# Conv columns of a streaming-encoder block moved from direct projections into seven-product units, with the recurrence two chunks at a time

## The chip, the cores and the metric

The kernel runs on one core of a Trainium2 chip. A core has TensorE (matmul, PE in the profile), VectorE (DVE), ScalarE (ACT), GpSimd (POOL) and SyncE (SP), which here issues nearly all DMAs; each engine takes its own instructions in order. The metric is the device time of one launch in microseconds: the median of three runs of the kernel before is 801.97 us (801.75 to 802.11).

## The reference

One block of a hybrid encoder on 512 frames of width 2048. The input is normalised, projected by one matrix, and split into nine parts. Four of them, 1024 columns each, make a gated short convolution; the others make a gated linear attention in chunks of 64 frames. Both results go through one output matrix, are added to the input and normalised again.

```python
h = rms_norm(x, norm_g)
ch, cb, cc, cz, gq, gk, gv, gr, gd = split(h @ w_in)   # 4 x 1024, 512, 512, 1024, 1024, 16
# short convolution: u = cc * ch, causal, 3 taps
y_conv = cb * (conv_b + sum(conv_w[j] * u[t - 2 + j])) * silu(cz)
# linear attention, 4 heads, chunks of 64 frames
glog = log_sigmoid(gd @ w_up + b_gate) / 16
b = cumsum(glog, within a chunk)
k_dec = gk * exp(b_end - b)
state = exp(b_end) * state + k_dec.T @ gv               # chunk after chunk
o = (gq / sqrt(128)) @ state                            # every frame reads its own chunk's state
y_gla = rms_norm(o, per head) * gla_norm_g * silu(gr)
out = rms_norm(x + concat(y_conv, y_gla) @ w_out) * final_g
```

## The kernel before, in words

All arithmetic is float32. Each matmul operand is split into a high part (a cast to the type TensorE multiplies) and a low part (the difference), and a product is three matmuls: high by high, low by high, high by low. ScalarE makes the high parts, VectorE the low ones (`split`, L117 to L119). A weight tile is 128 x 1024 elements (512 KB): it is loaded into one of eight raw buffers (`load_raw`, RAWBUFS = 8) and split into one of four pairs of high and low buffers (SPLITBUFS = 4). Small tiles of 128 x 512 come from one pool of 44 buffers (`t2`, `t2r`). PSUM has eight banks in two pools of four, `acc` and `aux`.

The stages, in order:

- *Token-major projection* (`tm`, L264): the decay gate's input, k and v, with frames on the partitions.
- *Projection units* (`ft_unit`): each makes 128 columns for 512 frames, with columns on the partitions: 16 blocks of the contraction x 3 matmuls = 48 matmuls of 512 columns, from two weight tiles. There are 28: four for q, sixteen for the first half of the conv columns (four blocks of z, b, c, h, `conv_block`), eight for r (`r_block`). After each half unit `step()` advances the generator `gla_steps`, which lays the recurrence in small pieces beside them, one chunk at a time: `chunk_state` (k and v put so that the high part of a chunk lies on 64 partitions and its low part on the other 64, so that one matmul adds both; then the state update and its split), two half units later `chunk_out` (q by the state). After each second chunk `out_norm` normalises a token tile and `out_transpose` turns it into the eight tiles `oT`. `r_block` multiplies silu(r) by `oT` and stores the product to `y_raw` in DRAM.
- *Quarter sums* (`quarter_sums`): for the seven-product units, sums and differences of quarters of the scaled input, four lots of two 512 KB loads, sixteen VectorE sums in all, split again; one lot each after r blocks 0, 2, 4 and 6. `place_third` puts one of the differences over a part of the input that is no longer read.
- *Seven-product units* (`st_unit`): a 512 x 1024 output block from seven products of half-size blocks in place of eight (products pa, pb, pc, then pd, pe, pa, pf in four rounds; 48 matmuls each, 336 in all). Three products take weights as they are, four take sums of weight tiles that VectorE makes (`mix`). Two such units make the second half of the conv columns, a third one, later, half of the output projection.
- *Output projection* (`po`, `part`), with the conv blocks of the second half transposed in between (`conv_tail`: eight transposes, then taps on ScalarE and VectorE), the third unit, and the final norm.

The program is written in one order; a scheduler then puts each engine's instructions into an order by its own estimates, so that a transpose or a split can stand among the matmuls of another stage. Buffers of the pools are handed out at that point too: a load waits until the buffer's last reader is done. Some names in the rows that follow: `hhi` and `hlo` are the high and low parts of the input, `raw_qx` the loads of the quarter sums, `qs` the sums, `qp` their splits, `c` the output tiles of a unit.

Of the kernel before, what the change touches and what calls it, by code (L numbers as in the profile page):

```python
# [13 lines left out]
P = 128  # L14
# [27 lines left out]
PRE = 4  # L42
# [8 lines left out]
def hybrid_block(ctx: ExitStack, tc: tile.TileContext, xT, x, params, w_tm, w_ft, w_st, w_up, b_gate, w_out, final_g, out):  # L51
# [57 lines left out]
    r2B = t2("r2B")  # L109
# [179 lines left out]
    nc.vector.tensor_mul(out=r2B, in0=rB, in1=rB)  # L289
# [58 lines left out]
    state = [None, None]  # L348

    def stack(src, rows, swap, name, both):  # L350

        a = t2r(f"{name}_a")
        nc.scalar.copy(out=a[rows, :], in_=src[rows, :])
        hi = a[rows, :].bitcast(F32)
        if not both:
            nc.vector.tensor_sub(out=a[swap, :], in0=src[rows, :], in1=hi)
            return a
        b = t2r(f"{name}_b")
        nc.scalar.copy(out=a[swap, :], in_=src[rows, :])
        nc.vector.tensor_sub(out=b[rows, :], in0=src[rows, :], in1=hi)  # L360
        nc.vector.tensor_sub(out=b[swap, :], in0=src[rows, :], in1=hi)
        return a, b

    split_state = [None, None]

    def chunk_state(n):
        tt, j = divmod(n, 2)
        rows = slice(j * CHUNK, (j + 1) * CHUNK)
        swap = slice((1 - j) * CHUNK, (2 - j) * CHUNK)
        kh, kl = stack(kv[tt][0], rows, swap, f"k{n}", True)  # L370
        for pr in range(2):
            vs = stack(kv[tt][1 + pr], rows, swap, f"v{n}_{pr}", False)
            u = aux(f"u{n}_{pr}")
# [5 lines left out]
            st = t2(f"s{n}_{pr}")  # L379
            if state[pr] is None:  # L380
                nc.vector.tensor_copy(out=st, in_=u)
            else:
                for i in range(2):
                    hh = 2 * pr + i
                    vsl = slice(i * HV, (i + 1) * HV)
                    nc.vector.scalar_tensor_tensor(
                        out=st[:, vsl], in0=state[pr][:, vsl], scalar=decay[:, hh, n : n + 1],
# [147 lines left out]
    for _ in steps:  # L535
        pass
# [503 lines left out]
```

## Time and profile before

| | us |
|---|---|
| median of 3 runs | 801.97 |
| the profiled execution | 801.89 |
| its span, first to last instruction | 799.7 |
| TensorE busy | 789.5 |
| VectorE busy | 514.6 |
| ScalarE busy | 352.4 |
| GpSimd busy | 38.1 |
| projection units with the recurrence, from 142 to 472 us of the span | 330 |
| first two seven-product units, 472 to 624 us | 152 |

Times in the profile are counted from the first instruction of the span. A matmul's listed duration (0.39 us for 512 columns) is longer than its step to the next one, since matmuls are pipelined; what one costs is read from the distance of starts. The same holds on VectorE and ScalarE by a little. A count after an x stands for instructions merged into one row.

### The profile page before, as it was taken

Reading aid. Unit: us, or ns where it says so; the run is one execution under the profiler, and the core shown is the slowest. Engines: PE = TensorE matmul, PEld = TensorE weight load, DVE = VectorE, ACT = ScalarE, POOL = GpSimd, SP = SyncE. Lnnn points to the kernel's source line nnn. Section 1 sums busy time; section 2 is a strip of 40 time slices with the busy share of each in tenths; the row PEclk is TensorE's granted clock in tenths of the full one; section 3 lists DMA queues with packets and bytes.
Section 4 is the critical chain, followed back from the end, with each engine's and each line's share of the span. In section 5 each row is a group of like instructions: output and inputs, shape, how many; then the busy total and the mean of one; then the engine's idle time right before and its main releaser. Section 6 shows DMA issues by size and latency. Waiting matters only on the chain.

```text
span 799.7 us, 9962 instructions
## 1 busy us (share of the span) xinstructions
PE 789.5 (99%) x3784; PEld 681.4 (85%) x3784; DVE 514.6 (64%) x672; ACT 352.4 (44%) x538; POOL 38.1 (5%) x42
## 2 busy tenths in 40 slices
PE   9999999999999999999999999999999999999996
PEld 9999999888888888788888888888888888888885
DVE  7543242465566566565555577969887998997923
ACT  6542212454445444455344355435445444644504
POOL 1000000000000000000000000000000000003601
PEclk9999999999999999999999999999999999999998
DMA  9963333322222222322355555564665359658105
GB/s 317 313 258 99 107 127 110 106 80 86 100 80 94 104 72 101 105 93 80 100 177 184 173 193 180 192 209 137 235 209 185 106 179 360 200 208 285 32 1 210
DMA packets 43171, 123.60 MB, mean 155 GB/s; under 512 B 5186, under 2 KB 7234, under 8 KB 43124
## 3 DMA queue, kind: packets, MB, share of 16 engines
q1 hardware_dynamic: 42868, 122.96, 45.4%
q8 instruction: 29, 0.48, 0.2%
q14 instruction: 18, 0.15, 0.1%
q10 hardware_dynamic: 256, 0.02, 0.0%
HBM read 115.61 MB, written 7.34 MB: 154 GB/s over the span
## 4 chain that ended last, share of the span: by engine, by line
PE 93%; issue 3%; DVE 1%; ACT 1%; POOL 0%; DMA 0%; ACTq 0%; POOLq 0%; DVEq 0%
PE tm L264 17%; PE ft L159 11%; PE ft L160 11%; PE ft L161 11%; PE pa L616 8%; PE pf L616 4%; PE pe L616 4%; PE pd L616 4%; PE pc L616 4%; PE pb L616 4%; PE po L159 3%; PE po L161 3%; PE po L160 3%; PE warm L87 1%; PE tp L433 0%
## 5 line engine op out<-in xcount | busy, mean ns | idle before, releaser
L159 PE MATMUL ft<-hhi,hi_ft 128*128 128x512 f32 x448 | 174.9, 390 | 0.0
L161 PE MATMUL ft<-hhi,lo_ft 128*128 128x512 f32 x448 | 174.7, 390 | 0.0
L160 PE MATMUL ft<-hlo,hi_ft 128*128 128x512 f32 x448 | 174.6, 390 | 0.0
L118 ACT CAST hi_ft<-raw_ft 128x1024 fp32r<-128x1024 f32 x56 | 58.9, 1052 | 120.0 <-PE ft L160 65.4
L119 DVE TENSOR_TENSOR lo_ft<-raw_ft,hi_ft 128x1024 fp32r<-128x1024 f32 x56 | 68.4, 1224 | 51.9 <-ACT hi_ft L118 51.5
L161 PEld LDWEIGHTS ft<-hhi,lo_ft 128*128 128x128 f32 x448 | 84.1, 188 | 17.5
L159 PEld LDWEIGHTS ft<-hhi,hi_ft 128*128 128x128 f32 x448 | 84.2, 188 | 17.0 <-issue 0.2
L160 PEld LDWEIGHTS ft<-hlo,hi_ft 128*128 128x128 f32 x448 | 84.2, 188 | 16.9
L118 ACT CAST hi_sq_t<-raw_sq 128x1024 fp32r<-128x1024 f32 x48 | 50.5, 1054 | 69.8 <-PE pa L616 14.9
L119 DVE TENSOR_TENSOR lo_sq_t<-raw_sq,hi_sq_t 128x1024 fp32r<-128x1024 f32 x48 | 59.5, 1244 | 15.2 <-ACT hi_sq_t L118 15.0
L665 DVE TENSOR_TENSOR raw_sq<-raw_sq,raw_sq 128x1024 f32<-128x1024 f32 x48 | 58.4, 1221 | 10.0 <-DMA raw_sq<-in_w_st 9.8
L119 DVE TENSOR_TENSOR lo_tm<-raw_tm,hi_tm 128x776 fp32r<-128x776 f32 x24 | 23.2, 966 | 58.4 <-ACT hi_tm L118 55.1
L118 ACT CAST hi_st<-raw_st 128x1024 fp32r<-128x1024 f32 x36 | 38.0, 1054 | 50.4 <-PE pb L616 14.7
L264 PE MATMUL tm<-hi_tm,hhi 128*128 128x388 f32 x256 | 56.5, 343 | 0.0
L264 PE MATMUL tm<-hi_tm,hlo 128*128 128x388 f32 x256 | 55.8, 340 | 0.0
L264 PE MATMUL tm<-lo_tm,hhi 128*128 128x388 f32 x256 | 55.4, 338 | 0.0
L119 DVE TENSOR_TENSOR lo_st<-raw_st,hi_st 128x1024 fp32r<-128x1024 f32 x36 | 43.6, 1222 | 15.5 <-ACT hi_st L118 15.3
L118 ACT CAST hi_tm<-raw_tm 128x776 fp32r<-128x776 f32 x24 | 20.2, 842 | 67.8 <-PE tm L264 64.5
L264 PEld LDWEIGHTS tm<-hi_tm,hhi 128*128 128x128 f32 x256 | 46.5, 190 | 0.0
L264 PEld LDWEIGHTS tm<-hi_tm,hlo 128*128 128x128 f32 x256 | 46.3, 189 | 0.0
L264 PEld LDWEIGHTS tm<-lo_tm,hhi 128*128 128x128 f32 x256 | 46.0, 188 | 0.0
L159 PE MATMUL po<-hi_wo,yh 128*128 128x512 f32 (+1 forms) x104 | 39.6, 381 | 0.0
(284 smaller groups left out, 1319.2 us busy)
## 6 DMA issues: line engine op xcount, KB each, us to landing
raw_ft<-in_w_ft SPq DMA_DIRECT2D x56, 512.0 KB, 3.3
raw_sq<-in_w_st SPq DMA_DIRECT2D x32, 512.0 KB, 3.7
raw_st<-in_w_st SPq DMA_DIRECT2D x24, 512.0 KB, 3.9
raw_tm<-in_w_tm SPq DMA_DIRECT2D x24, 388.0 KB, 5.0
raw_sq<-in_w_out SPq DMA_DIRECT2D x16, 512.0 KB, 4.2
raw_wo<-in_w_out SPq DMA_DIRECT2D x13, 512.0 KB, 3.8
raw_st<-in_w_out SPq DMA_DIRECT2D x12, 512.0 KB, 8.2
rawx<-in_xT SPq DMA_DIRECT2D x16, 256.0 KB, 4.8
```

The costliest lines, as they stand in the source:

```text
L87: nc.tensor.matmul(wps[:, 0:P], lhsT=ones, rhs=ones, start=True, stop=True)
L118: nc.scalar.copy(out=hi, in_=full)
L119: nc.vector.tensor_sub(out=lo, in0=full, in1=hi.bitcast(F32))
L159: nc.tensor.matmul(ps, lhsT=ah, rhs=bh, start=first, stop=False)
L160: nc.tensor.matmul(ps, lhsT=ah, rhs=bl, start=False, stop=False)
L161: nc.tensor.matmul(ps, lhsT=al, rhs=bh, start=False, stop=last)
L264: nc.tensor.matmul(pst[tt][:, 0:TMC], lhsT=a[:, tt * P : (tt + 1) * P], rhs=w, start=kt == 0 and k == 0, stop=kt == KT - 1 and k == 2,)
L616: nc.tensor.matmul(ps[t], lhsT=fs[t][part_], rhs=ww[:, sl], start=first and c == 0 and r == 0 and k == 0, stop=last and c == STC - 1 and r ...
L665: nc.vector.tensor_tensor(out=dst, in0=x0, in1=x1, op=op)
```

## The change

All 4096 conv columns now go through seven-product units: four of them, two for each half (w_st is laid out for four; `st_source` takes w_st for u < 4). `conv_block` and its sixteen projection units are gone, so that twelve projection units are left, q and r. The first half's conv blocks are finished by `early_tail`, inside the third unit, in the two banks that this unit uses later for pd; the transposes and taps of both halves share `conv_transposed`.

The recurrence handles two chunks in one step: `chunk_splits` splits a whole 128-frame tile of k and v; `pair_state` multiplies each chunk on its own 64 partitions with three matmuls per head; `pair_out` makes both chunks' output and the norm, whose scaling has moved from VectorE to ScalarE. It runs beside q and r alone. Since `oT` isn't ready when r is, `r_block` stores silu(r) to `r_raw` in DRAM; `gated_rows`, after the first unit, loads it, multiplies by `oT` and stores to `y_raw`. All four quarter sums stand behind r blocks 6 and 7.

```diff
-    def stack(src, rows, swap, name, both):
...
-    def chunk_state(n):
...
+    def chunk_splits(tt):
+        kv_split[tt] = [split_small(kv[tt][j], f"kv{tt}_{j}") for j in range(3)]
+
+    def pair_state(tt):
+        kp = kv_split[tt][0]
         for pr in range(2):
+            vp = kv_split[tt][1 + pr]
+            us = [aux(f"u{2 * tt + j}_{pr}") for j in range(2)]
             for i in range(2):
                 hh = 2 * pr + i
                 ksl, vsl = slice(hh * HK, (hh + 1) * HK), slice(i * HV, (i + 1) * HV)
-                nc.tensor.matmul(u[:, vsl], lhsT=kh[:, ksl], rhs=vs[:, vsl], start=True, stop=False)
-                nc.tensor.matmul(u[:, vsl], lhsT=kl[:, ksl], rhs=vs[:, vsl], start=False, stop=True)
...
+                for k, (a, b) in enumerate(((0, 0), (0, 1), (1, 0))):
+                    for j in range(2):
+                        rows = slice(j * CHUNK, (j + 1) * CHUNK)
+                        nc.tensor.matmul(
+                            us[j][:, vsl], lhsT=kp[a][rows, ksl], rhs=vp[b][rows, vsl], start=k == 0, stop=k == 2
+                        )
+            for j in range(2):
...
+                state[pr] = st
+                split_state[n, pr] = split_small(st, f"sp{n}_{pr}")
...
+    def pair_out(tt):
+        o = [t2(f"o{tt}_{pr}") for pr in range(2)]
+        for j in range(2):
+            chunk_out(2 * tt + j, o)
+        out_norm(tt, o)
+        return o
...
-                nc.vector.tensor_scalar(
-                    out=o[pr][:, vsl], in0=o[pr][:, vsl], scalar1=ro[:, hh : hh + 1], scalar2=None, op0=ALU.mult
-                )
+                nc.scalar.activation(o[pr][:, vsl], o[pr][:, vsl], AF.Copy, scale=ro[:, hh : hh + 1])
...
+        chunk_decays()
+        chunk_splits(0)
         yield
...
-        for n in range(NCH):
-            chunk_state(n)
+        for tt in range(TT):
+            pair_state(tt)
             if done is not None:
-                out_transpose(*done)
-                done = None
+                out_transpose(tt - 1, done)
             yield
+            if tt + 1 < TT:
+                chunk_splits(tt + 1)
             yield
...
+            done = pair_out(tt)
             yield
...
+    def gated_rows(n):
+        raw = raw_tile(f"yg{n}")
+        for k in range(2):
+            half = raw[:, k * S : (k + 1) * S]
+            nc.sync.dma_start(out=half, in_=r_raw[2 * n + k])
+            nc.vector.tensor_mul(out=half, in0=half, in1=oT[2 * n + k])
+            nc.sync.dma_start(out=y_raw[FB + 2 * n + k], in_=half)
...
-    def conv_block(fb):
...
     def r_block(b):
-        r = ft_unit(HEADS + 2 * FB + b)
+        r = ft_unit(HEADS + b)
...
-        nc.vector.tensor_mul(out=t1, in0=t1, in1=oT[b])
-        nc.sync.dma_start(out=y_raw[FB + b], in_=t1)
+        nc.sync.dma_start(out=r_raw[b], in_=t1)
...
-    for fb in range(PRE):
-        conv_block(fb)
...
     for b in range(8):
         r_block(b)
-        if b % 2 == 0:
-            quarter_sums(b // 2)
+        if b >= 6:
+            for j in range(2):
+                quarter_sums(2 * (b - 6) + j)
+    for _ in steps:
+        pass
...
+        pd = [main(f"pd{u}_{t}") for t in range(2)]
+        for f in between[:2]:
+            f(pd)
         p2 = [side(f"pb{u}_{t}") for t in range(2)]
         raw_mm(p2, "a12", B21)
         add(c11, p2)
         out(0, 0, c11)
+        for f in between[2:]:
+            f(pd)
...
+    def conv_transposed(f, fb, tu, tg, yy, uc, gz):
+        fsl = slice(f * P, (f + 1) * P)
+        for tt in range(TT):
+            nc.tensor.transpose(out=tu[:, tt * P : (tt + 1) * P], in_=uc[tt][:, fsl], identity=ident)
+        for tt in range(TT):
+            nc.tensor.transpose(out=tg[:, tt * P : (tt + 1) * P], in_=gz[tt][:, fsl], identity=ident)
+        conv_taps(yy, tu, fb)
+        nc.vector.tensor_mul(out=yy, in0=tg, in1=yy)
+
+    def early_tail(f):
+        made = list(uc), list(gz)
+
+        def go(banks):
+            yy = t2(f"yc{f}")
+            conv_transposed(f, f, *banks, yy, *made)
+            nc.sync.dma_start(out=y_raw[f], in_=yy)
+
+        return go
+
+    st_unit(0, h_factor, gate_cols, ahead_of(1))
+    for n in range(4):
+        gated_rows(n)
+    st_unit(1, h_factor, conv_cols, ahead_of(2))
+    st_unit(2, h_factor, gate_cols, ahead_of(3), between=[early_tail(f) for f in range(4)])
+    st_unit(3, h_factor, conv_cols, next_stage)
```

What this does to the order of instructions is shown at three places. The first is TensorE where a chunk's u (its new part of the state) is made. Before, one chunk's u for two heads stands between two projection units (`v_0_a` is the v tile with high and low part on the two halves, `k_a` and `k_b` the k tiles):

```order
L161 MATMUL ft_1809<-hhi_120,lo_ft_1_1843 128x512
L377 MATMUL u_0_1879<-v_0_a,k_a 128x256
L378 MATMUL u_0_1879<-v_0_a,k_b 128x256
L377 MATMUL u_0_1879<-v_0_a,k_a 128x256
L378 MATMUL u_0_1879<-v_0_a,k_b 128x256
L159 MATMUL ft_1907<-hhi_117,hi_ft_0_1910 128x512
```

Now the u's of two chunks stand there (u_0_1870 and u_0_1871), in twos on the lower and the upper 64 partitions:

```order
L159 MATMUL ft_1761<-hhi_119,lo_ft_1_1843 128x512
L363 MATMUL u_0_1870<-kv_1_hi,kv_0_hi 128x256
L363 MATMUL u_0_1871<-kv_1_hi,kv_0_hi 128x256
L363 MATMUL u_0_1870<-kv_1_lo,kv_0_hi 128x256
L363 MATMUL u_0_1871<-kv_1_lo,kv_0_hi 128x256
L363 MATMUL u_0_1870<-kv_1_hi,kv_0_lo 128x256
L363 MATMUL u_0_1871<-kv_1_hi,kv_0_lo 128x256
L363 MATMUL u_0_1870<-kv_1_hi,kv_0_hi 128x256
```

The run of four has become a run of 24, of which the first seven are shown, and the chunks alternate.

The second place is VectorE from the evacuation of r block 6 on, just ahead of the first seven-product unit. Before:

```order
L119 TENSOR_TENSOR lo_st_0_0_3919<-raw_st_0_0_3916,hi_st_0_0_3918 128x1024
L516 TENSOR_TENSOR r_6_3815<-ft_3754,rB 128x512
L553 TENSOR_TENSOR qs_3_3828<-raw_qx_3820,raw_qx_3824 128x512
L119 TENSOR_TENSOR lo_st_1_0_3937<-raw_st_1_0_3934,hi_st_1_0_3936 128x1024
L518 TENSOR_TENSOR r_6_3815<-r_6_3815,oT_1682 128x512
L553 TENSOR_TENSOR qs_3_3830<-qs_3_3828,raw_qx_3820 128x512
L119 TENSOR_TENSOR hlo_121<-qs_0_3354,hhi_117 128x2x256
L553 TENSOR_TENSOR qs_3_3832<-raw_qx_3824,qs_3_3830 128x512
L553 TENSOR_TENSOR qs_3_3834<-raw_qx_3820 128x512
L119 TENSOR_TENSOR hlo_121<-qs_1_3514,hhi_117 128x2x256
L154 TENSOR_TENSOR qp_3_lo<-qs_3_3832,qp_3_hi 128x512
L119 TENSOR_TENSOR lo_st_2_0_3955<-raw_st_2_0_3952,hi_st_2_0_3954 128x1024
```

Now:

```order
L493 TENSOR_TENSOR r_6_2676<-ft_2615,rB 128x512
L525 TENSOR_TENSOR qs_0_2688<-raw_qx_2680,raw_qx_2684 128x512
L525 TENSOR_TENSOR qs_0_2690<-qs_0_2688,raw_qx_2680 128x512
L525 TENSOR_TENSOR qs_0_2692<-raw_qx_2684,qs_0_2690 128x512
L525 TENSOR_TENSOR qs_0_2694<-raw_qx_2680 128x512
L152 TENSOR_TENSOR qp_0_lo<-qs_0_2692,qp_0_hi 128x512
L117 TENSOR_TENSOR hlo_120<-qs_0_2694,hhi_116 128x2x256
L152 TENSOR_TENSOR qp_0_lo<-qs_0_2688,qp_0_hi 128x512
L152 TENSOR_TENSOR qp_0_lo<-qs_0_2690,qp_0_hi 128x512
L525 TENSOR_TENSOR qs_1_2716<-raw_qx_2708,raw_qx_2712 128x512
L525 TENSOR_TENSOR qs_1_2718<-qs_1_2716,raw_qx_2708 128x512
L117 TENSOR_TENSOR lo_st_0_0_2862<-raw_st_0_0_2859,hi_st_0_0_2861 128x1024
```

`lo_st_0_0` to `lo_st_3_0` are the low parts of the unit's first four weight tiles. The first stood ahead of r block 6's evacuation and the second behind one sum; now six sums and four low parts stand between that evacuation and the first, and the sums read `raw_qx` buffers that the weight tiles are loaded into next.

The third place is TensorE in the third unit, between its products pa and pb, where before no transposes stood. Now, at the end of the first early block's transposes and the start of the second's (`pd` is the pair of banks, `c_1` and `c_0` the unit outputs):

```order
L591 MATMUL pa_0_4041<-lo_st_3_0_4088,hhi_117 128x512
L591 MATMUL pa_1_4042<-lo_st_3_0_4088,hhi_117 128x512
L732 MATMUL pd_1_4108<-ident,c_0_1_2932 128x128
L732 MATMUL pd_1_4108<-ident,c_0_0_3403 128x128
L732 MATMUL pd_1_4108<-ident,c_0_1_3404 128x128
L591 MATMUL pb_0_4137<-hi_st_0_2_4141,hhi_118 128x512
```

and, sixteen pb matmuls after these three transposes,

```order
L591 MATMUL pb_1_4138<-hi_st_1_2_4159,hlo_122 128x512
L730 MATMUL pd_0_4107<-ident,c_1_0_3537 128x128
L730 MATMUL pd_0_4107<-ident,c_1_1_3538 128x128
L730 MATMUL pd_0_4107<-ident,c_1_0_3999 128x128
L730 MATMUL pd_0_4107<-ident,c_1_1_4000 128x128
L591 MATMUL pb_0_4137<-lo_st_1_2_4160,hhi_118 128x512
```

The second block's transposes into pd_0 come 16 matmuls after the first block's last ones into pd_1.

## Rows read from the trace of the kernel before

**Rows 1.** The page, part 1: busy us, share of the span and instructions of each engine.

```profile
PE 789.5 (99%) x3784; PEld 681.4 (85%) x3784; DVE 514.6 (64%) x672; ACT 352.4 (44%) x538; POOL 38.1 (5%) x42
```

**Rows 2.** The page, part 4: shares by engine of the chain that ended last.

```profile
PE 93%; issue 3%; DVE 1%; ACT 1%; POOL 0%; DMA 0%; ACTq 0%; POOLq 0%; DVEq 0%
```

**Rows 3.** Waits of TensorE: total us, times, longest.

```profile
PE u L377 <- DVE v_a L356: 1.2, 1, 1.2
```

**Rows 4.** Busy time by stage: window, length, busy us of each engine, clock, DMA share, GB/s.

```profile
142.00:472.00 330.00, 328.84 (x1528) 273.72 (x1527) 195.36 (x275) 153.73 (x262) 10.77 (x8) 1.00 0.33 111
472.00:548.00 76.00, 76.00 (x337) 62.96 (x336) 57.58 (x55) 35.28 (x40) 0.00 (x0) 1.00 0.58 191
548.00:624.00 76.00, 76.00 (x337) 62.96 (x336) 64.81 (x65) 38.19 (x43) 0.00 (x0) 1.00 0.55 187
...
671.00:747.50 76.50, 76.50 (x339) 63.38 (x338) 70.52 (x75) 40.20 (x54) 10.71 (x6) 1.00 0.69 235
```

**Rows 5.** TensorE timeline, 45 matmuls of a projection unit, first and last: start, us, what.

```profile
439.81 0.39 PE L159 MATMUL ft<-hhi,hi_ft 128*128 128x512 f32 x1
...
449.78 0.39 PE L161 MATMUL ft<-hhi,lo_ft 128*128 128x512 f32 x1
```

**Rows 6.** The chain in order of time: start, us, what; one product of a seven-product unit.

```profile
482.81 10.88 PE pb L616 x48
```

**Rows 7.** TensorE timeline: four u matmuls and the two after them.

```profile
189.65 0.28 PE L377 MATMUL u<-v_a,k_a 128*128 128x256 f32 x1
...
190.12 0.40 PE L159 MATMUL ft<-hhi,hi_ft 128*128 128x512 f32 x1
190.36 0.40 PE L160 MATMUL ft<-hlo,hi_ft 128*128 128x512 f32 x1
```

**Rows 8.** TensorE timeline: the first of 16 transposes, the two matmuls after them.

```profile
634.98 0.60 PE L800 MATMUL tu<-ident,c 128*128 128x128 f32 x4
...
636.64 0.48 PE L159 MATMUL po<-hi_wo,yh 128*128 128x512 f32 x1
636.95 0.40 PE L160 MATMUL po<-lo_wo,yh 128*128 128x512 f32 x1
```

**Rows 9.** TensorE timeline: a full-height matmul, then the 8-row transposes.

```profile
183.40 0.39 PE L161 MATMUL ft<-hhi,lo_ft 128*128 128x512 f32 x1
183.72 0.41 PE L339 MATMUL dp<-ident,dec 8*128 8x8 f32 x4
```

**Rows 10.** VectorE by line and shape: busy us and mean ns, idle before and releaser.

```profile
L386 DVE SCALAR_TENSOR_TENSOR s<-s,decay,u 128x256 f32<-128x256 f32 x28 | 12.2, 476 | 6.1 <-PE u L378 6.1
...
L154 DVE TENSOR_TENSOR sp_lo<-s,sp_hi 128x512 fp32r<-128x512 f32 x16 | 11.0, 689 | 7.6 <-ACT sp_hi L153 7.6
```

**Rows 11.** ScalarE by line and shape.

```profile
L118 ACT CAST hi_ft<-raw_ft 128x1024 fp32r<-128x1024 f32 x56 | 58.9, 1052 | 120.0 <-PE ft L160 65.4 <-DMA raw_ft<-in_w_ft 21.9 <-issue 19.7
...
L118 ACT CAST hi_st<-raw_st 128x1024 fp32r<-128x1024 f32 x36 | 38.0, 1054 | 50.4 <-PE pb L616 14.7 <-PE pa L616 8.6 <-issue 8.1
...
L153 ACT CAST sp_hi<-s 128x512 fp32r<-128x512 f32 x16 | 9.9, 621 | 22.3 <-DVE s L386 19.1 <-DVE s L381 3.2
...
L405 ACT COPY ol<-o 64x512 f32<-64x512 f32 x16 | 8.5, 583 | 0.1
...
L412 ACT ACTIVATE junk<-o 128x256 f32<-128x256 f32 x16 | 6.7, 416 | 3.4 <-DVE o L406 3.1
...
L412 ACT ACTIVATION_READ_ACCUMULATOR junk<-o 128x1 f32 x16 | 3.0, 187 | 0.0
```

**Rows 12.** VectorE timeline: six adds in a row, five low parts in a row.

```profile
545.66 3.67 DVE L643 TENSOR_TENSOR c<-c,pa 128x512 f32<-128x512 f32 x6
...
553.44 5.76 DVE L119 TENSOR_TENSOR lo_st<-raw_st,hi_st 128x1024 fp32r<-128x1024 f32 x5
```

**Rows 13.** POOL by line and shape: the power for the output norm.

```profile
L419 POOL TENSOR_TENSOR ro<-mso,nhalf 128x4 f32<-128x4 f32 x4 | 4.0, 1012 | 93.5 <-DVE mso L417 93.5
```

**Rows 14.** DMA issues: count, KB each, median us from issue to landing.

```profile
raw_st<-in_w_st SPq DMA_DIRECT2D x24, 512.0 KB, 3.9
```

More of the change, by code (lines that the diff above doesn't have):

```diff
@@ L41 @@
 WARM = 9
-PRE = 4
 K2BUFS = 44
@@ L423, in out_norm @@
                 vsl = slice(i * HV, (i + 1) * HV)
-                nc.vector.tensor_scalar(
-                    out=o[pr][:, vsl], in0=o[pr][:, vsl], scalar1=ro[:, hh : hh + 1], scalar2=None, op0=ALU.mult
-                )
+                nc.scalar.activation(o[pr][:, vsl], o[pr][:, vsl], AF.Copy, scale=ro[:, hh : hh + 1])
     def out_transpose(tt, o):
+        if not oT:
+            oT.extend(t2(f"oT{b}") for b in range(8))
         for pr in range(2):
@@ L483, in hybrid_block @@
     y_raw = keep.tile([KT, P, S], F32, name="y_raw")
+    r_raw = keep.tile([FB, P, S], F32, name="r_raw")
+    def gated_rows(n):
[5 more added lines that the diff above has]
+            nc.sync.dma_start(out=y_raw[FB + 2 * n + k], in_=half)
     def conv_taps(yy, u, fb):
@@ L620, in product, with st_unit @@
                     )
-    def st_unit(u, factor, out, before_out, into=None):
+    def st_unit(u, factor, out, before_out, into=None, between=()):
         main, side = (aux, acc) if u % 2 else (acc, aux)
@@ L657, in st_unit @@
         c12 = kept(p3, 0, 1)
-        p5 = [main(f"pd{u}_{t}") for t in range(2)]
+        p5 = pd
         p7 = [side(f"pe{u}_{t}") for t in range(2)]
@@ L734, in wo_weights, with ahead_of, go @@
         return wo_ahead[cbk, c]
-    def next_unit():
-        for c in range(2):
-            st_weights(1, c, B11)
+    def ahead_of(u):
+        def go():
+            for c in range(2):
+                st_weights(u, c, B11)
+        return go
     def next_stage():
@@ L796, in conv_tail @@
         fb = FB // 2 + f
-        fsl = slice(f * P, (f + 1) * P)
-        tu, tg = (aux if f % 2 else acc)(f"tu{f}"), (aux if f % 2 else acc)(f"tg{f}")
-        for tt in range(TT):
-            nc.tensor.transpose(out=tu[:, tt * P : (tt + 1) * P], in_=uc[tt][:, fsl], identity=ident)
-        for tt in range(TT):
-            nc.tensor.transpose(out=tg[:, tt * P : (tt + 1) * P], in_=gz[tt][:, fsl], identity=ident)
         n, k = divmod(fb, 2)
@@ L935, in last_stage @@
                 load_gain(cbk)
-    st_unit(2, y_factor, res_cols, last_stage, into=lambda i, j, t: res[2 * i + t][1 + j])
+    st_unit(4, y_factor, res_cols, last_stage, into=lambda i, j, t: res[2 * i + t][1 + j])
     for tt in range(TT):
@@ L987, in blocks @@
         return a.reshape(KT, P, -1, P).transpose(2, 1, 0, 3)
-    half = CONV // 2
-    conv = np.stack([blocks(a[:, :, :half]) for a in (cz, cbb, cc, ch)], axis=1).reshape(2 * FB, P, KT, P)
     def unit(left, right):
-        a = np.stack([left[:, :, half:], right[:, :, half:]])
-        a = a.reshape(2, 2, STC, 2, P, S).transpose(2, 1, 0, 4, 3, 5)
+        a = np.stack([left, right]).reshape(2, 2, STC, 2, P, S).transpose(2, 1, 0, 4, 3, 5)
         return a.reshape(STC, 4, P, 2 * S)
-    st = np.stack([unit(cz, cbb), unit(cc, ch)])
-    ft = np.concatenate([blocks(q), conv, blocks(r)], axis=0)
+    halves = [slice(0, S), slice(S, 2 * S)]
+    st = np.stack([unit(a[:, :, s], b[:, :, s]) for s in halves for a, b in ((cz, cbb), (cc, ch))])
+    ft = np.concatenate([blocks(q), blocks(r)], axis=0)
     ft = ft.reshape(-1, P, 2, D // 2).transpose(0, 2, 1, 3)
```

94 lines of the change are left out of this document (21 added, 73 removed).

## The prediction

> **What bounds the kernel now.** I read the busy line of the page first [rows 1]: TensorE is busy 789.5 of 799.7 us, VectorE 514.6, ScalarE 352.4. A busy TensorE need not be a bound one, so the chain that ended last comes next [rows 2]: 93% of it is TensorE. Then its waits [rows 3]: before the tail it waited once for work, 1.2 us for a stacked v tile. And the table by stage [rows 4]: in the projections with the recurrence it has 328.84 of 330.00 us, in each seven-product unit all of the window. So time is what TensorE is given to do, plus whatever it is made to wait. VectorE is the one near it: 57.6, 64.8 and 70.5 of about 76 us in the three units, and still TensorE waits for nothing there.
>
> **Prices on TensorE.** In the projection units 45 matmuls start from 439.81 to 449.78 us, 44 steps of 0.2266 us [rows 5]; in a seven-product unit 48 take 10.88 us, 0.2267 each [rows 6]. The two stages cost the same per matmul, so here only the count matters. A run of four u matmuls (256 columns) takes 189.65 to 190.12 us, 0.117 each [rows 7]. Sixteen transposes take 634.98 to 636.64 us, 0.104 each, and the matmul behind them takes 0.31 instead of 0.23 to its successor; with that hand-over a run of 16 is 1.75 us, 0.109 each [rows 8].
>
> **The change part by part.** (1) Conv columns. Sixteen projection units of 48 matmuls go: 768. Two seven-product units of 7 x 48 = 336 come: 672. Net 96 fewer, 96 x 0.2267 = -21.8 us. This is the whole gain.
>
> (2) Recurrence, u. Before, high and low part lay on the two halves of the partitions, so 8 chunks x 2 x 4 = 64 matmuls over 128 rows did the sum. Now each chunk stays on its own 64 rows and three products are issued one by one: 4 pairs x 24 = 96. One after the other at 0.117 that is +3.7 us. Side by side, two chunks at a time, it would be 48 x 0.117, which is -1.9 us against before. No row shows two matmuls on different halves of the rows, so these are the two ends. I take +3.7, because a transpose streams half the columns of a u matmul and costs nearly as much (0.109 against 0.117): the price of these short ones is not that of the columns that stream. Half-height and full-height matmuls also alternate now. The nearest row is the 8-row transposes of the decays: from the full-height matmul before them to their start it is 0.32 us in place of 0.23 [rows 9], 0.09 more. The u's stand in six runs (three for the first pair of chunks), so 12 switches, 0 to 0.1 each; I take +1.1.
>
> The Trainium skill, "TensorEngine Tiling (Array Packing)", section "Key Properties", says both that tiles on different rows work in parallel and that a change of the tiling mode drains the engine. No row here shows the first; the 0.09 us agrees with a small drain at most.
>
> (3) Transposes of the four early conv blocks: 4 x 8 x 0.109 = +3.5 us. They stand in seven runs among other matmuls, each with a hand-over of 0.09, so +0.5 more. All four blocks use the same two banks, so each waits for the taps of the one before; that is under (5).
>
> (4) The 1.2 us wait for a stacked v tile goes with the stacking: -1.2. What is late next are the waits of (5).
>
> Sum without new waits: -21.8 + 3.7 + 1.1 + 3.5 + 0.5 - 1.2 = -14.2 us.
>
> (5) New waits, by places; none can be less than nothing. **Recurrence beside q and r.** A pair of chunks now passes in three half units. From the first u to the first o TensorE has 24 u and 48 projection matmuls, 2.8 + 10.9 = 13.7 us. The state needs half the u's (1.4 us), then four times two updates (0.48 each), a cast (0.62) and a low part (0.69) [rows 10, 11], 9.0 us, and VectorE passes two projection splits in between (1.14 us each by the pitch of a run of five [rows 12]): 12.7 us. It fits by 1 us. The norm is closer: in the second pair only 10 projection matmuls, 24 u and 3 more (5.8 us) stand between the last o and the first transpose of the normed output. On ScalarE two copies (0.58), four squares (0.42 + 0.19 for the accumulator) and a split (1.05) come to 4.6; then 1.01 on POOL [rows 13] and the scaling, now on ScalarE, not shown there before, by the square's shape 0.42: 6.1 us and hand-overs. That is 0.5 to 1 us late. I take 1.5 for all four pairs, 0 to 6 as range.
> **Start of the first unit.** All four quarter sums now stand behind r blocks 6 and 7, and eight of their 512 KB loads hold all eight raw buffers. The first weights of the unit get a buffer only when VectorE has made four sums after the end of r block 6: 0.2 + 0.69 + 4 x 0.605 = 3.3 us (0.605 by the run of six [rows 12]). Landing 3.9 [rows 14], cast 1.05, low part 1.14: ready at 9.5, wanted at 10.9. The unit's third and fourth weight tiles wait for the next sums (10.1 us): 10.1 + 3.9 + 1.05 + 1.14 and hand-overs make 16.4 to 17.4, wanted at 10.9 + 5.4 = 16.3. So TensorE waits about 1 us there; SP has r block 6's store ahead of those loads, which waits for the same evacuation and costs nothing more. After that VectorE catches up by my count. I take 1.5, range 0 to 5.
> **Early conv tails.** The second block's transposes want the bank whose taps come behind a weight split on VectorE: after the product, 0.3 of transposes, cast 1.05, low part 1.14, two taps by the adds' pitch 0.605 each, with hand-overs 4.0 to 4.5 us; TensorE has 3 transposes and 16 matmuls, 4.0. For both such places together 0.8, range 0 to 3.
> **DRAM round trip of silu(r).** Eight stores more, eight loads, eight products (4.8 us of VectorE) at the end of the first unit. SP's stores wait for VectorE and the next unit's third weight load stands behind them. It is wanted 5 us into that unit, so nothing; if it is late by one landing, 3.9 us. Range 0 to 4; I take 0.6.
> Two more units bring VectorE and ScalarE no new pace: the third one has the second's 64.8 us plus tails of 4 x 3 x 0.605, 72.1 of 80, 90%; that is the share of the last unit, 92%, which costs TensorE nothing [rows 4]. Loads keep a unit's pace too, 0.55 to 0.58 of the DMA engines [rows 4]. What the direct conv blocks did on VectorE, ScalarE and POOL goes at no gain, since TensorE waited for none of it.
> Waits: 1.5 + 1.5 + 0.8 + 0.6 = 4.4.
>
> **Sum.** -14.2 + 4.4 = -9.8 us. Against the profiled execution, span 799.7 and 2.2 around it, that is 792.1; the median of the runs, 801.97, stands 0.08 above the profiled one: 792.2 us.
>
> **Rivals.** (A) The half-height u's run side by side: 5.6 us less for u, 786.6 us. For it: neighbours alternate between halves of the rows and write different banks. Against: the short matmuls' price of (2). Chance 0.2. By the rule of the Trainium skill named under (2), that tiles on different rows work in parallel, (A) is what would come.
> (B) The recurrence's chain comes too late for o. In a pair of chunks it has 16 hand-overs between VectorE and ScalarE, and 1 us of margin by (5). If each is 0.3 us longer than I count, that is 4.8 us a pair, 3.8 beyond the margin, 15.2 in four pairs: 807 us, slower than before. It decides from 9.8 us of waits more, 2.5 a pair, 0.22 on each hand-over. For it: the queues are in order, so one late operand delays everything behind it, and ScalarE's load grows beside it (scaling of o, sixteen scalings of x for the quarter sums). Against: before, the chain of every chunk had the same hand-overs, and TensorE waited 1.2 us in all [rows 3]. Chance 0.08.
> (C) VectorE becomes the bound in the first unit. To its 57.6 us [rows 4] come 8 gated products, 16 sums, 12 low parts and 4 placements, 40 x 0.605 = 24.2, and of r block 7's stretch the evacuation and three weight splits, 4.1: 85.9 us of work in 10.9 + 76.2 = 87.1. If VectorE stands still for 7 of these us, waiting for loads or casts, TensorE ends the unit 6 us later: 798 us. For it: before, it had 18 us of pauses there. Against: those were for want of work, and by my count its lead over TensorE grows from 1 to 3 us in the first two products. Chance 0.15.
> (D) The waits don't come at all: 787.8 us. It lies in the forecast's own range.
>
> **How the numbers follow.** Forecast 792.2 (0.57), (A) 786.6 (0.2), (C) 798 (0.15), (B) 807, with all that ends over 800 (0.08). About 0.2% is what a measurement of this kernel can tell from no change, here 800.4 to 803.6. The forecast alone runs from 787 (no waits) to 797. The range of 8 in 10: (A) without waits is 782; above, (C) with some of the forecast's upper waits reaches 799.5. Chances: faster 0.87, same 0.06, slower 0.07.
>
> **What would show it.** The count: 576 projection and 1680 unit matmuls at 0.2267. The u's: a run of 24 taking 2.8 us (mine) or 1.4 (A). TensorE's waits: rows for the normed output's transposes, for the third weight tile of the first unit, for the second early block's transposes, some 4 us together. Wrong if the idle time of TensorE before the tail is over 10 us, if a unit takes more than 78 us without transposes in it, or if the granted clock falls in the middle of the span.

## The result, and the profile after

| | before | after |
|---|---|---|
| median of the runs, us | 802.0 (801.75 to 802.11) | 791.16 (790.61 to 792.51) |
| ratio, 95% interval | | 0.9868 (0.9851 to 0.9885) |
| profiled execution; its span | 801.89; 799.7 | 790.9; 788.9 |

Forecast were 792.2 us and a range of 782 to 799.5. The total came 1.0 us below the forecast, but two of its terms were wrong, in opposite directions. The busy line of the page after, to be held against [rows 1]:

```profile
PE 772.4 (98%) x3752; PEld 663.4 (84%) x3752; DVE 564.7 (72%) x711; ACT 379.9 (48%) x574; POOL 31.2 (4%) x38
```

TensorE has 17.1 us less to do, and the span is only 10.8 shorter: 6.3 us of idle time are new. TensorE's waits after (engine, line, waited for; us in total, times, longest), beside [rows 3]:

```profile
PE tp L429 <- ACT o L420: 4.5, 4, 1.9
PE tp L429 <- ACT oT L432: 1.4, 1, 1.4
...
PE pa L591 <- DVE lo_st L117: 0.7, 1, 0.7
```

The 1.2 us for the stacked v is gone. In its place come 5.9 us for the normed output and 0.7 us for a weight tile. By stage, as in [rows 4] (window, length, busy us of PE, PEld, DVE, ACT, POOL, clock, DMA share, GB/s): the projections with the recurrence, then the four units.

```profile
142.30:303.70 161.40, 155.43 (x789) 127.25 (x789) 96.56 (x149) 102.81 (x207) 4.04 (x4) 1.00 0.28 89
303.70:379.90 76.20, 76.20 (x338) 63.06 (x338) 72.29 (x82) 41.07 (x51) 0.00 (x0) 1.00 0.82 271
379.90:457.00 77.10, 76.44 (x337) 62.98 (x336) 63.88 (x65) 34.62 (x39) 0.00 (x0) 1.00 0.66 223
457.00:537.00 80.00, 80.00 (x369) 65.95 (x368) 69.69 (x75) 37.40 (x43) 0.00 (x0) 1.00 0.60 197
537.00:613.30 76.30, 76.30 (x338) 63.20 (x337) 65.17 (x65) 38.69 (x43) 0.00 (x0) 1.00 0.56 186
```

All the idle time is in the first stage and, 0.7 us, at the start of the second unit. A product still takes what it took in [rows 6]; the chain in order of time has

```profile
402.79 10.88 PE pc L591 x48
```

The u's, in the second pair of chunks, on TensorE's timeline (start, length of the row, line, what; x2 means two instructions of one row). The four u's of [rows 7] took 0.117 us each:

```profile
205.57 0.38 PE L363 MATMUL u<-kv_hi,kv_hi 64*128 64x256 f32 x2
205.80 0.28 PE L363 MATMUL u<-kv_lo,kv_hi 64*128 64x256 f32 x2
205.91 0.28 PE L363 MATMUL u<-kv_hi,kv_lo 64*128 64x256 f32 x2
...
206.98 0.29 PE L363 MATMUL u<-kv_hi,kv_lo 64*128 64x256 f32 x2
207.20 0.50 PE L157 MATMUL ft<-hhi,hi_ft 128*128 128x512 f32 x1
```

Two matmuls, one on each half of the rows, take a step of 0.119 us together; the run of 24 lasts 1.63 us (205.57 to 207.20), not the 2.8 I had forecast. Rival (A) is right on this point. The Trainium skill, "TensorEngine Tiling (Array Packing)", section "Key Properties", says that tiles on different rows work in parallel; the trace agrees, 0.119 us for two.

What follows there on ScalarE, GpSimd and TensorE (the bracket is the idle time before, and what ended it):

```profile
205.21 0.42 ACT L408 ACTIVATE junk<-o 128x256 f32<-128x256 f32 x1 [0.50 <-DVE o L395]
...
205.62 1.04 ACT L116 CAST hi_ft<-raw_ft 128x1024 fp32r<-128x1024 f32 x1
...
207.96 0.19 ACT L408 ACTIVATION_READ_ACCUMULATOR junk<-o 128x1 f32 x1
209.52 1.71 ACT L420 ACTIVATE o<-o,ro 128x256 f32<-128x256 f32 x4 [1.37 <-POOL ro L415]
```

```profile
208.47 1.02 POOL L415 TENSOR_TENSOR ro<-mso,nhalf 128x4 f32<-128x4 f32 x1 [152.54 <-DVE mso L413]
```

```profile
210.08 0.44 PE L429 MATMUL tp<-ident,o 128*128 128x128 f32 x2 [1.92 <-ACT o L420]
```

This is the place that the prediction named for the norm, with the weight split between the squares. It named 0.5 to 1 us of lateness; 1.92 came. The u's are part of what TensorE has to do in the meantime: 24 of them in 1.6 us in place of 2.8 give 1.2 us less cover. Three of the four pairs have their u's in that place.

### The profile page after: what moved, and what is told of

Read it like the earlier page. It is cut to its first block, busy times and chain, and to the rows that moved or that the text cites. A ratio compares the mean times of both kernels' runs of the same rounds, so it can differ in the third digit from the quotient of the medians.

```text
span 788.9 us, 10098 instructions
## 1 busy us (share of the span) xinstructions
PE 772.4 (98%) x3752; PEld 663.4 (84%) x3752; DVE 564.7 (72%) x711; ACT 379.9 (48%) x574; POOL 31.2 (4%) x38
## 5 line engine op out<-in xcount | busy, mean ns | idle before, releaser
L116 ACT CAST hi_sq_t<-raw_sq 128x1024 fp32r<-128x1024 f32 x80 | 84.2, 1055 | 118.5 <-PE pa L591 24.9
L117 DVE TENSOR_TENSOR lo_sq_t<-raw_sq,hi_sq_t 128x1024 fp32r<-128x1024 f32 x80 | 98.6, 1236 | 22.0 <-ACT hi_sq_t L116 21.8
L645 DVE TENSOR_TENSOR raw_sq<-raw_sq,raw_sq 128x1024 f32<-128x1024 f32 x80 | 97.0, 1219 | 5.6 <-DMA raw_sq<-in_w_st 4.7
L157 PE MATMUL ft<-hhi,hi_ft 128*128 128x512 f32 x192 | 75.8, 395 | 0.0
L158 PE MATMUL ft<-hlo,hi_ft 128*128 128x512 f32 x192 | 75.4, 392 | 0.0
L159 PE MATMUL ft<-hhi,lo_ft 128*128 128x512 f32 x192 | 75.2, 392 | 0.0
L117 DVE TENSOR_TENSOR lo_ft<-raw_ft,hi_ft 128x1024 fp32r<-128x1024 f32 x24 | 29.4, 1224 | 25.4 <-ACT hi_ft L116 25.4
L157 PEld LDWEIGHTS ft<-hhi,hi_ft 128*128 128x128 f32 x192 | 36.1, 188 | 7.6 <-issue 0.2
L159 PEld LDWEIGHTS ft<-hhi,lo_ft 128*128 128x128 f32 x192 | 36.1, 188 | 7.6
L158 PEld LDWEIGHTS ft<-hlo,hi_ft 128*128 128x128 f32 x192 | 36.1, 188 | 7.0
```

The costliest lines, as they stand in the source:

```text
L116: nc.scalar.copy(out=hi, in_=full)
L117: nc.vector.tensor_sub(out=lo, in0=full, in1=hi.bitcast(F32))
L157: nc.tensor.matmul(ps, lhsT=ah, rhs=bh, start=first, stop=False)
L158: nc.tensor.matmul(ps, lhsT=ah, rhs=bl, start=False, stop=False)
L159: nc.tensor.matmul(ps, lhsT=al, rhs=bh, start=False, stop=last)
L645: nc.vector.tensor_tensor(out=dst, in0=x0, in1=x1, op=op)
```

## The experiments

Each kernel was run beside the kernel before on the same chip; its ratio is to that kernel.

**1. The norm's wait: is it time?** In the generator:

```diff
             pair_state(tt)
-            if done is not None:
-                out_transpose(tt - 1, done)
             yield
+            if done is not None:
+                out_transpose(tt - 1, done)
...
             done = pair_out(tt)
             yield
+        yield
         out_transpose(TT - 1, done)
```

> The changed kernel, but the transposes of a pair's normed output stand one half unit later (24 projection matmuls, 5.4 us), the last pair's too. In the changed kernel TensorE waits 5.9 us before such transposes, at most 1.9 at once. Theory (the norm's chain is late by just these waits, and they are time): the rows of waits for the normed output go and the four waits are not replaced; 791.2 - 5.9 = 785.3 us. Rival (the chain is a pipeline without slack: what is not waited for here is waited for at the next u or o): 791 us, with 4 to 6 us of waits before u or o.

785.49 us (785.33 to 786.85), ratio 0.9799 (0.9786 to 0.9812): 5.7 us below the change. TensorE's waits for work in its profile (the profiled run is the longest of the five, 786.85 us):

```profile
PE pa L592 <- DVE lo_st L117: 1.4, 1, 1.4
...
PE o L391 <- ACT oT L432: 0.7, 1, 0.7
```

The rows for the normed output are gone, and one short wait for a bank (o behind oT) is new. The waits were time, and 5.4 us more work ahead of the transposes is enough to remove them. The kernels below, but for 2 and 3, are built on this one.

**2. Is it the scaling on ScalarE?**

```diff
-                nc.scalar.activation(o[pr][:, vsl], o[pr][:, vsl], AF.Copy, scale=ro[:, hh : hh + 1])
+                nc.vector.tensor_scalar(out=o[pr][:, vsl], in0=o[pr][:, vsl],
+                    scalar1=ro[:, hh : hh + 1], scalar2=None, op0=ALU.mult)
```

> The changed kernel with the scaling of the normed output back on VectorE. Theory (what is late is the whole chain of two copies, four squares, a split, POOL's power; the scaling is its last small step, 0.85 us before the first transposes can go): waits for the normed output fall by 0 to 0.4 us a pair, 790 to 791.2 us. Rival (the waits are there because the scaling went to ScalarE, behind its other work): they fall from 5.9 to under 2 us, 787 us or less.

791.72 us (789.93 to 794.8), ratio 0.9881 (0.9863 to 0.9899): no gain, and the rival's 787 us or less did not come. The waits, 6.8 us, are on the other engine, 4.7 for the scaled output and 2.1 for a state update (s):

```profile
PE tp L431 <- DVE o L420: 4.7, 3, 1.8
PE tp L431 <- DVE s L375: 2.1, 1, 2.1
```

**3. Does the wait belong to the schedule of pairs?** The kernel before, with `pair_state`, `pair_out`, `chunk_splits`, the scaling and the generator of the change; the units untouched. In the generator:

```diff
-        for n in range(NCH):
-            chunk_state(n)
+        for tt in range(TT):
+            pair_state(tt)
             if done is not None:
-                out_transpose(*done)
-                done = None
-            yield
+                out_transpose(tt - 1, done)
             yield
...
+            done = pair_out(tt)
             yield
```

> The kernel before, with the recurrence by pairs of chunks alone (the scaling on ScalarE with it); conv columns, r, stores and quarter sums as before. Theory (the late norm belongs to the schedule of pairs, three half units each): 802.0 - 1.2 (stacked v) - 0.2 (u) + 0.9 (transposes in more runs) + 5.9 (waits) = 807 us, slower than before. Rival (the waits come from what stands beside the recurrence in the changed kernel, r blocks and quarter sums): no waits, 801.5 us.

808.29 us (807.5 to 809.02), ratio 1.0082 (1.0069 to 1.0095): 6.6 us slower than before, so this half of the change alone costs time, and the other half (two units for sixteen projection units, with the early tails), with the sums moved and the gated rows, is worth 808.3 - 791.2 = 17.1 us. The waits are those of the whole change:

```profile
PE tp L433 <- ACT o L424: 5.5, 4, 1.9
...
PE tp L433 <- ACT oT L436: 0.6, 1, 0.6
```

The profile shows a second price, which I had not expected. TensorE's timeline behind the longest wait:

```profile
209.56 0.44 PE L433 MATMUL tp<-ident,o 128*128 128x128 f32 x2 [1.90 <-ACT o L424]
...
211.42 0.63 PE L160 MATMUL ft<-hlo,hi_ft 128*128 128x512 f32 x1
211.85 0.63 PE L161 MATMUL ft<-hhi,lo_ft 128*128 128x512 f32 x1
212.27 0.63 PE L159 MATMUL ft<-hhi,hi_ft 128*128 128x512 f32 x1
```

and the stretches around it (columns as above; the 1.00, 0.50 and 0.94 are the granted clock):

```profile
206.00:210.00 4.00, 2.10 (x20) 1.45 (x17) 2.08 (x4) 2.57 (x10) 1.02 (x1) 1.00 0.34 128
...
211.90:213.60 1.70, 1.70 (x6) 1.31 (x5) 1.02 (x4) 0.62 (x1) 0.00 (x0) 0.50 0.00 0
213.60:216.00 2.40, 2.40 (x14) 2.00 (x13) 1.71 (x4) 0.62 (x1) 0.00 (x0) 0.94 0.00 0
```

After a wait of 1.9 us seven projection matmuls start 0.43 us apart and not 0.2266, at half the clock (1.2 GHz): 7 x 0.2 = 1.4 us, some 1.6 with the two steps beside them, on top of the wait. In the profile of the change no matmul does this, after a wait of the same length.

**4. The u's on one half of the rows.** All chunks read the upper rows (partitions 0 to 63); the second chunk's own rows are left out of the computation:

```diff
                     for j in range(2):
-                        rows = slice(j * CHUNK, (j + 1) * CHUNK)
+                        rows = slice(0, CHUNK)
```

> As late_transposes, but the u's of both chunks read the upper 64 rows (so the second chunk's state is made from the first chunk's rows; this part of the computation is changed). Number, shape and order of the matmuls are as in late_transposes. Theory (a matmul over 64 rows costs 0.119 us for its 256 columns like one over 128, and two run side by side only on different halves): no pairs any more, a run of 24 lasts 24 x 0.119 = 2.86 us in place of 1.63, 48 x 0.119 = 5.7 us in all; 785.5 + 5.7 = 791.2 us. Rival (half the rows, half the price, 0.06 each wherever they lie): 785.5 us, runs of 1.63 us.

789.76 us (788.16 to 791.16), ratio 0.9851 (0.9834 to 0.9868): 4.3 us more than late_transposes. The run of 24 in its timeline:

```profile
206.32 0.50 PE L363 MATMUL u<-kv_hi,kv_hi 64*128 64x256 f32 x2
206.66 0.39 PE L363 MATMUL u<-kv_lo,kv_hi 64*128 64x256 f32 x2
206.89 0.40 PE L363 MATMUL u<-kv_hi,kv_lo 64*128 64x256 f32 x2
...
209.37 0.50 PE L157 MATMUL ft<-hhi,hi_ft 128*128 128x512 f32 x1
```

Two now take 0.238 us, the run 3.05 (2.86 and the hand-over). The price of a matmul over 64 rows is thus that over 128, as I had it, and the gain comes from the two halves. Of the 5.7 us that I expected, the u's show 4.8 in the two profiles: in late_transposes the scheduler put the third pair's u's into two runs of 12, in fives and sixes on one half, and these take 1.13 and 1.47 us where 12 in turns take 0.91. The two spans differ by less, 3.0 us: the wait of o behind oT (0.7) is gone here, that for the weight tile is 0.9 in place of 1.4, and 0.6 I cannot place.

**5. The order of the u's.** First the loops over chunk and product exchanged, so that three stand on one half, then three on the other; then twelve and twelve:

```diff
-                for k, (a, b) in enumerate(((0, 0), (0, 1), (1, 0))):
-                    for j in range(2):
+                for j in range(2):
+                    for k, (a, b) in enumerate(((0, 0), (0, 1), (1, 0))):
...
+        for j in range(2):                # u_twelve_by_twelve: chunk outermost
+            for pr in range(2):
+                for i in range(2):
+                    for k, (a, b) in enumerate(((0, 0), (0, 1), (1, 0))):
```

> As late_transposes, and the u matmuls of one pair of heads are issued chunk after chunk (12 on the upper 64 rows, then 12 on the lower 64) and not in turns; counts, weights and columns are the same. To be compared with late_transposes, since in the changed kernel the u's lie ahead of a wait that would hide their price. Theory (two matmuls on different halves of the rows run side by side, 0.119 us for both): now nearly every one takes 0.119 alone, a run of 24 lasts 2.8 us instead of 1.63, and the kernel is 96 x 0.119 - 48 x 0.119 = 5.7 less a few pairs at the seams, 5 us longer than late_transposes. Rival (a matmul over 64 rows costs half of one over 128, in any order): no change, run of 24 at 1.63 us.

786.04 us (784.91 to 787.13), ratio 0.9804 (0.9791 to 0.9817): no change, against my theory, and the run of 24 is 1.62 us as before. The expectation speaks of twelve and twelve, but the edit makes groups of three, so it tests less than was expected of it. Neither side of that pair of expectations holds: experiment 4 rules out the rival. Started strictly in order, only the last of one group and the first of the next could run side by side, at the seven seams of eight groups: 24 - 7 = 17 steps, an estimated 2.2 us with the hand-over. So the queue does not stop at a matmul whose half is busy:

> As late_transposes, with the 24 u's of a pair issued as 12 on the upper rows, then 12 on the lower. With three by three (late_and_u_by_chunk) the run of 24 stayed at 1.63 us. Theory (each half of the rows takes its matmuls on its own, and TensorE's queue is read some few instructions ahead of what runs): twelve in a row on one half are further than that, so most of each twelve runs alone; the run of 24 is 2.2 to 2.8 us, 788 to 791 us. Rival (the order plays no part at all): 1.63 us and 785.5 us.

787.89 us (787.13 to 788.77), ratio 0.9829 (0.9814 to 0.9844): 2.4 us more than late_transposes. Its timeline, in which the first to twelfth u read the upper rows and the thirteenth is the first on the lower (a row of two gives the start of its first):

```profile
206.38 0.38 PE L363 MATMUL u<-kv_hi,kv_hi 64*128 64x256 f32 x1
...
207.43 0.28 PE L363 MATMUL u<-kv_hi,kv_lo 64*128 64x256 f32 x1
207.44 0.39 PE L363 MATMUL u<-kv_hi,kv_hi 64*128 64x256 f32 x2
207.66 0.29 PE L363 MATMUL u<-kv_lo,kv_hi 64*128 64x256 f32 x2
207.78 0.28 PE L363 MATMUL u<-kv_hi,kv_lo 64*128 64x256 f32 x2
207.90 0.28 PE L363 MATMUL u<-kv_hi,kv_hi 64*128 64x256 f32 x1
...
209.06 0.50 PE L157 MATMUL ft<-hhi,hi_ft 128*128 128x512 f32 x1
```

The ninth starts at 207.43. The tenth is due 0.12 us later, at 207.55, since on one half they start 0.12 apart (experiment 4); so the start at 207.44 is the thirteenth's. It is ahead of the tenth, eleventh and twelfth. These run beside the thirteenth to fifteenth, then nine on the lower rows run alone: 2.68 us. In all three runs of 24 the thirteenth starts 1.06 us behind the first. So in this run a matmul passed three that stood ahead of it in the queue and no more, enough for groups of three and not for twelve. That each engine takes its own instructions in order, as I wrote ahead of the prediction, does not hold for these matmuls.

**6. The quarter sums.** Four places for them, each a kernel of its own on top of late_transposes, in the loop over r blocks (after: two behind block 6, two behind 7):

```diff
-        if b >= 6:
-            for j in range(2):
-                quarter_sums(2 * (b - 6) + j)
+        if b >= 4:                                         # late_and_sums_spread
+            quarter_sums(b - 4)
+        if b % 2 == 0:                                     # late_and_sums_as_before
+            quarter_sums(b // 2)
+        for j in {4: (0,), 5: (1,), 6: (2, 3)}.get(b, ()): # late_sums_4566
+            quarter_sums(j)
+        if 3 <= b < 7:                                     # late_sums_3456
+            quarter_sums(b - 3)
```

> As late_transposes, with the four quarter sums behind r blocks 4, 5, 6 and 7, one each, and not two behind 6 and two behind 7. Theory (the first unit's third weight tile is late because all eight raw buffers hold the x tiles of the sums): the wait there (0.7 us in the changed kernel, 1.4 in late_transposes, none in the kernel with u by chunk) goes or stays under 0.3; 784 to 785 us. Rival (VectorE is simply behind, with the same work in the same stretch): the wait stays, 785.5 us.

786.79 us (786.07 to 787.43), ratio 0.9815 (0.98 to 0.9829). The wait stayed at 1.5 us. I had misread it, and the next expectations too speak of a wait "at the first unit": a row of waits names a line, not a unit. TensorE's timeline of the change has its time:

```profile
387.74 0.73 PE L591 MATMUL pa<-lo_st,hhi 128*128 128x512 f32 x2 [0.66 <-DVE lo_st L117]
```

The first unit begins at 303.7 us and the second at 379.9; this is the second unit's third weight tile, which the sums have long left behind (experiment 7).

> As late_transposes, with the quarter sums behind r blocks 0, 2, 4 and 6, where the kernel before had them. Theory: the wait at the first unit goes as in late_and_sums_spread, but the sums of the first three now stand beside the recurrence, with 2.5 us of scaling on ScalarE and 5 us on VectorE each; with the transposes later there is room for it, so 784 to 785 us. Rival (the recurrence has no room for it): 2 to 4 us of waits for o or the normed output, 787 to 789 us.

790.12 us (789.26 to 791.43), ratio 0.9858 (0.9843 to 0.9873): 4.6 us more than late_transposes; the rival's direction, and more than it gave. Beside the recurrence there are now waits for banks, for o and for the normed output, 2.8 us:

```profile
PE o L391 <- ACT oT L432: 1.5, 1, 1.5
...
PE tp L429 <- ACT o L420: 0.8, 1, 0.8
PE u L363 <- DVE o L395: 0.5, 1, 0.5
```

But late_transposes waits 2.1 us too (experiment 1). More goes to the half clock, here behind the shortest of these waits and some u's:

```profile
256.33 0.35 PE L363 MATMUL u<-kv_hi,kv_hi 64*128 64x256 f32 x1 [0.49 <-DVE o L395]
...
259.17 0.62 PE L158 MATMUL ft<-hlo,hi_ft 128*128 128x512 f32 x1
...
266.06 0.40 PE L157 MATMUL ft<-hhi,hi_ft 128*128 128x512 f32 x1
```

From 259.17 to 266.06 us eleven projection matmuls and a run of 12 u's take 6.9 us; by their steps at full clock (0.31 + 0.91 + 0.33 + 9 x 0.2267) I estimate 3.6, so 3.3 are lost. That is this profile, the longest of the four runs (791.43 us, mean granted clock 0.993). The other three, 789.26 to 790.29 us at 0.996 to 0.998, have no trace, and what the sums cost them is not shown.

> As late_transposes, with one quarter sum behind r block 4, one behind 5 and two behind 6, none behind 7. In late_and_sums_spread the wait at the first unit stayed at 1.5 us, with VectorE busy without a pause from 298.8 to 309 us, the last sum's seven operations between the low parts of the weights. Theory (it is the sum behind block 7 that delays the low parts, not the raw buffers): no wait at the first unit, 784.0 us. Rival (raw buffers held by the x tiles): a wait of 0.7 us or more stays, 785 us.

785.67 us (784.64 to 787.77), ratio 0.9807 (0.9793 to 0.9821): the same as late_transposes. Its profile, of its shortest run (784.64 us), has no wait for a weight tile, but its median does not follow; a wait that differs from run to run would do that.

> As late_transposes, with one quarter sum behind each of r blocks 3, 4, 5 and 6. Theory: as late_sums_4566 at the first unit (no wait); block 3's sum stands beside the last pair of chunks, and with the sums behind blocks 0, 2 and 4 the recurrence lost some 6 us, so 0 to 2 us are lost there: 784 to 786 us. Rival (any sum beside the recurrence costs it 2 us a piece): 786 us or more.

788.73 us (787.79 to 788.98), ratio 0.9836 (0.9822 to 0.985): 3.2 us more, by one sum beside the last pair; the rival is right here. Its waits:

```profile
PE tp L429 <- ACT o L420: 3.1, 1, 3.1
```

Behind it eight matmuls run at half the clock, which costs 1.6 us more. So that the change gathers the sums behind the recurrence was worth a few us (on top of late_transposes), an edit in which I had seen a cost alone.

**7. The gated rows.** Their loads, products and stores into the second unit; then left out:

```diff
-    for n in range(4):
-        gated_rows(n)
-    st_unit(1, h_factor, conv_cols, ahead_of(2))
+    st_unit(1, h_factor, conv_cols, ahead_of(2),
+            between=[lambda _, n=n: gated_rows(n) for n in range(4)])
...
-        nc.sync.dma_start(out=r_raw[b], in_=t1)           # late_no_gating, with no gated_rows
+        nc.sync.dma_start(out=y_raw[FB + b], in_=t1)
```

> As late_transposes, with the loads, products and stores of the gated rows inside the second unit (behind its first and second product), not at the seam between the first and the second. TensorE's wait for low_st named the line only; by its time (383.4 us in late_transposes, 387.7 in the changed kernel) it lies at the third weight tile of the second unit, not of the first, so the quarter sums could not remove it. Theory (at the seam VectorE has eight gated products, fourteen adds and four scalings between the weights' low parts, and waits for the loads of silu(r) in order): the wait of 0 to 1.4 us goes, 784.5 us, and the runs lie within 1 us of each other. Rival (the products delay the weights wherever they stand): 785.5 us, with a wait inside the second unit.

785.11 us (784.9 to 785.54), ratio 0.979 (0.9776 to 0.9803), the lowest median, but by 0.4 us, less than the runs of late_transposes differ. No wait for a weight tile in its profile, and its five runs lie within 0.64 us of each other, where those of late_transposes lie within 1.5.

> As late_transposes, with silu(r) stored straight as the gated rows: no second trip and no products with the normed output (this part of the computation is left out). Theory (the trip costs TensorE the wait at the seam of the first two units and nothing else): 784.5 us, no wait there. Rival (its 4 MB of traffic also slow the weights' loads in the first unit, where the DMA engines are busy 0.82 of the time in the changed kernel): 783 us or less.

785.54 us (785.15 to 785.91), ratio 0.9796 (0.9783 to 0.9809): with no trip at all the time is that of late_transposes. The trip costs the median nothing that can be told. At the seam of the first two units the profiles with the trip there show a wait of 0 to 1.5 us; the two kernels without it there show none, in one profile each. VectorE's timeline at the end of the first unit in the change shows how the trip can bring it:

```profile
368.08 0.69 DVE L478 TENSOR_TENSOR raw_yg<-raw_yg,oT 128x512 f32<-128x512 f32 x1 [1.15 <-DMA raw_yg<-r_raw]
...
371.42 0.69 DVE L478 TENSOR_TENSOR raw_yg<-raw_yg,oT 128x512 f32<-128x512 f32 x1 [1.52 <-DMA raw_yg<-r_raw]
...
383.82 2.73 DVE L691 SCALAR_TENSOR_TENSOR c<-c,rstd,c 128x512 f32<-128x512 f32 x4
386.47 5.76 DVE L117 TENSOR_TENSOR lo_st<-raw_st,hi_st 128x1024 fp32r<-128x1024 f32 x5
```

It waits 2.7 us for loads of silu(r), in order, is from then on busy without a pause, and reaches the low part for TensorE's next weight tile only at 386.47.

## Why the prediction was right in sum, and where not

Terms measured from the two profiles; "excess" is the distance of the projection or unit matmuls around a run of short ones less their own steps.

| step | forecast | measured |
|---|---|---|
| (1) 96 matmuls fewer | -21.8 | -21.8 (96 steps of 0.2267) |
| (2) u, with switches | +4.8 | about +0.3 |
| (3) early transposes | +4.0 | about +3.8 |
| (4) stacked v | -1.2 | -1.2 |
| (5) recurrence and norm | 1.5 | 5.9 |
| (5) start of the first unit | 1.5 | 0 |
| (5) early conv tails | 0.8 | 0 |
| (5) trip of silu(r) | 0.6 | 0.7 in the profile, 0 to 1.5 in others |
| not named: normed output's transposes in 11 runs, not 4 | 0 | about +1.0 |

The measured terms sum to -11.3, the span fell by 10.8; of the 0.5 us between them 0.2 are an earlier stage, the rest I cannot place.

**Right.** The count (1) is the whole gain, and the two stages still cost the same per matmul. The place of the new wait was right to the instruction. Rivals (B) and (C) did not come: no wait for o or u in the change; in the first unit VectorE was busy for 72.3 of 76.2 us and TensorE never waited.

**Wrong: step (2).** The error was to price the u's one after another, from the nearest row of short matmuls, and to give rival (A) the lesser chance. The transposes told how much a short matmul costs, and that was right (experiment 4: 0.119 alone); they told nothing of two at once. The hand-overs were under-sized too: a run of 24 takes 1.63 us, 12 x 0.119 = 1.43 and 0.2 more, the step into it is 0.31 and the matmul behind it takes 0.33 to its successor. That is 0.4 us a run, 2.3 for six runs, where I had 1.1. So the u's, though side by side, take 8.2 us in all, against 7.8 before.

**Wrong: step (5), the norm.** Mostly a consequence of the first error. I held the chain (6.1 us and hand-overs) against 5.8 us of TensorE's work, 2.8 of them u's; at 1.6 for the u's the work is 4.6, and the wait 1.2 longer. Of the waits of 1.92, 1.64 and 0.34 us behind the three runs of 24 that makes 1.2, 1.2 and all of the last, 2.7 of the 4.4 us that the term is short. The 1.4 us for the bank that oT still holds I had not seen. This is worked out, not run: no kernel has u's one after another ahead of the early transposes. By it more than half of the 4.5 us that the u's won against my forecast was lost right behind them. That the rest cancelled to 1.0 us is luck: 2.3 us of other waits did not come, and the bank (1.4) and the transposes in more runs (1.0) came unforeseen. Had I taken (A) for (2), I would have forecast 786.6 and been 4.6 us off. With the wait out of the way (experiment 1) 785.5 us is reached.

**Wrong, with little weight:** the two places at which I had counted margins of about 1 us in units; both held.

**Open.** The runs of the change spread over 1.9 us, those of the kernel before over 0.4. The wait at the seam (0 to 1.5 us) and the half clock after a wait (1.6) would both do that. The mean granted clock, which every run has, tells something of the second: it is 0.996 to 0.998 in all runs of the kernel before and of late_transposes (every profile has some half clock in the tail), but 0.994 in one run of the change (791.42 us), and in scale_on_vector 0.992 to 0.994 in the three longer runs (792.61 to 794.8) and 0.997 in the other three (789.93 to 790.82). So the half clock very likely comes in runs without a trace too, but it is not the whole spread: the longest run of the change (792.51) is at 0.996. The wait at the seam shows in profiled runs alone.

## What to carry to other kernels

When a term shortens what TensorE does between a producer and its consumer, the wait behind it has to be worked out again with the shorter cover: a saving and a wait next to each other are one term, not two. Matmuls over half the rows should be priced by two ends, alone and side by side, and issued so that neighbours in the queue, by these runs within about three places, lie on different halves. A wait's row names a line; its time, from the timeline, says which of the line's places it is.

## What the runs showed of the hardware

- Two matmuls over 64 rows each, on different halves, take 0.119 us for both at 256 columns; on the same half 0.238. Groups of three on a half cost nothing against strict turns; groups of twelve cost 1.05 us a run, and there the thirteenth started ahead of the tenth to twelfth.
- After a wait of TensorE of 1.9 us (experiment 3) and 3.1 us (late_sums_3456) the granted clock fell from 1.00 to 0.50 (1.2 GHz), and seven and eight projection matmuls took 0.43 us a step before it rose again. In late_and_sums_as_before it fell behind a wait of 0.49 us and some u's, and was at 0.50 up to 266 us. After a wait of 1.92 us in the change the clock stayed at 1.00. What decides is not shown by these runs.
